# A transformer layer with 32 experts on one core: weights stored in the order of their tiles

## The chip, the core and the metric

One core of one Trainium2 chip. Its engines work beside each other and meet through semaphores: TensorE (PE, matmuls, with PEld for its weight loads), VectorE (DVE), ScalarE (ACT), GpSimd (POOL) and SyncE (SP, which here issues the transfers). Sixteen DMA engines carry data from the chip's memory (HBM) to the core's own memory. The metric is device time in microseconds.

## The reference

One layer of a diffusion transformer in float32: 256 latent tokens and 256 context tokens of width 1024. It is adaLN, two attention branches with their gates, and then a mixture of experts: the four best of 32 experts for each token.

```
def ada_params(cond, w_ada, b_ada):
    m = jax.nn.silu(cond) @ w_ada + b_ada
    return jnp.split(m, N_MOD, axis=-1)
...
def hybrid_layer(x, ctx, mod, mod_ctx, p, rope, update_ctx):
    shift1, scale1, gate1, shift2, scale2, gate2 = mod
...
    k_mla_c, v_mla_c, k_swa_c, v_swa_c = kv_side(hc, p, None)
    k_mla, v_mla, k_swa, v_swa = kv_side(h, p, rope)
    q_mla, q_swa, gate_a, gate_b = q_side(h, p, rope)
    o_a = mla_attend_latent(q_mla, k_mla, v_mla, k_mla_c, v_mla_c)
    o_b = swa_attend_latent(q_swa, k_swa, v_swa, k_swa_c, v_swa_c, p['swa_sink'])
    x_new = x + gate1[..., None, :] * merge_branches(o_a, o_b, gate_a, gate_b, p)
    x_new = x_new + gate2[..., None, :] * moe(modulate(x_new, p['norm2_g'], shift2, scale2), p)
...
def moe(h, p):
...
    def run_block(args):
        tok, e, w = args
        xb = x_pad[tok]
        act = clamped_swiglu(xb @ w_gu[e] + b_gu[e])
        return (act @ w_dn[e] + b_dn[e]) * w[:, None]
```

An expert holds a gate-and-up matrix of 1024 x 2048 and a down matrix of 1024 x 1024, 12.6 MB in float32; the 32 experts are 403 MB. The attention part reads some 55 MB more.

## The kernel before

The kernel has a **front** (adaLN, keys, values and queries, attention, merge, router) and then the 32 **experts**, each with all its weights and at most 64 tokens. Weights land in ten **frames** of 128 partitions x 4096 float32 (`frames`, in the profile `f`; a frame that gets new contents in its second life is called `g`). In the experts the load of a **slab** fills one frame: 512 rows of a matrix by 1024 columns, 2048 KB. Nine frames go round in a fixed order, `order = (2, 7, 3, 6, 8, 4, 5, 9, 1)`; an expert takes four slabs of the gate-and-up matrix and two of the down matrix. The first slabs come in two halves each (`parts=2`), and the last expert's down matrix in smaller pieces.

In memory the matrices stand row by row. A load takes rows `k0*128 ...` of some columns and puts row `k*128 + p` into partition p, so that what a partition gets is several separate runs:

```
def kslab(f, lo, w, k0, kn, c0, cn):
    return load(f, lo, w[k0 * 128:(k0 + kn) * 128, c0:c0 + cn].rearrange("(k p) n -> p k n", p=128), kn, cn)
```

A run is `cn` columns: 1024 (4 KB) in the experts' slabs, 512 (2 KB) for the output projection and for adaLN beside attention, 256 (1 KB) for the branch projections, 128 (512 B) for the gates and for the adaLN pieces of the head. In the head, adaLN comes in eight pieces `a0` to `a7` of 1 MB (two loads each), and the first columns of the input projection in pieces `v` and `q` of 256 KB. Beside attention, `ada_load` puts each of seven adaLN blocks into frame 4 (`f_67` in the order below) in two halves, DVE accumulates each with eight instructions, and `gate_load` and `br_load` put gate and branch weights into frames 2 and 3 (`f_65` and `f_66`).

The order of all instructions is found by `Program`, a list scheduler: the program is recorded in an order that is right, each instruction has a price in `price`, and the instruction with the longest path behind it goes first. It also chooses the engine of copies, scalings and subtractions that more than one engine can do (`either`). A load's price is its bytes divided by a constant. All loads are issued by SP in the order in which they were recorded, and a load that has to wait for its frame holds the loads behind it.

Of the kernel before, what the change touches and what calls it, by code (L numbers as in the profile page):

```python
# [18 lines left out]
D = 1024  # L19
# [3 lines left out]
H = 8  # L23
# [9 lines left out]
class View:  # L33
    """A tile that gets its place when the program is put in order, and the view taken of it."""
# [31 lines left out]
class Place:  # L66
    """A place on chip for new contents: its tile is made when the first instruction that touches it is issued."""
# [10 lines left out]
class Program:  # L78
    """Records the instructions of a program in an order that is right, and issues them in one that keeps every
    dependence and lets no engine wait without need: list scheduling by critical path on modelled engines."""  # L80
# [21 lines left out]
    def pool(self, slots, shared=False, ahead=8):  # L102
        """Places handed out as the order of issue is found; shared: tiles with other uses later on."""
        me = {"slots": slots, "free": [(0.0, s) for s in slots], "queue": [], "head": 0, "turn": 0, "shared": shared, "ahead": ahead}
        self.pools.append(me)
        uid = len(self.pools)

        def get():
            if self.direct:
                me["turn"] += 1  # L110
                return me["free"][me["turn"] % len(me["free"])][1]
            v = Virtual(me, f"v{uid}_{len(me['queue'])}")
            v.index = len(me["queue"])
            me["queue"].append(v)
            return View(v)

        return get
# [50 lines left out]
    def cells(self, x):  # L168
        """The tile of an access and the cells of it that it may touch."""
# [41 lines left out]
    def price(self, eng, method, args, kw):  # L211
# [3 lines left out]
        if eng == "sync":  # L215
            ap = self.concrete(out)
            b = 4
            for d in ap.shape:
                b *= d
            return b / 360.0  # L220
# [95 lines left out]
    # ---- ordering  # L316
    def order(self):
# [11 lines left out]
        def work(s, cost):  # L329
            """End of tensor engine work that starts at s: half speed in a window after one with little work."""  # L330
# [125 lines left out]
def emit(nc, tc, io, out):  # L456
# [7 lines left out]
    # ---------------------------------------------------------------- places on chip  # L464
# [34 lines left out]
    def load(f, lo, src, a, b):  # L499
        v = fv(f, lo, a * b, a)  # L500
        SY.dma_start(v, src)
        return v

    def kslab(f, lo, w, k0, kn, c0, cn):
        return load(f, lo, w[k0 * 128:(k0 + kn) * 128, c0:c0 + cn].rearrange("(k p) n -> p k n", p=128), kn, cn)
# [59 lines left out]
    # split of float32 into two float32r parts that add up to it exactly  # L565
# [29 lines left out]
    # ---------------------------------------------------------------- loads of the head  # L595
    def ada_head_load(k):
        v = fv(2 + k // 2 % 3, k % 2 * 2048, 2048)
        w = v.rearrange("p (i k n) -> p i k n", i=2, k=KT)
        for i in range(2):
            SY.dma_start(w[:, i], io["w_ada"][:, i * D + k * 128:i * D + (k + 1) * 128].rearrange("(k p) n -> p k n", p=128))  # L600
        return w
# [4 lines left out]
    def head_load(what):  # L606
# [5 lines left out]
        elif a in "vq":  # L612
            kslab({"v": 5, "q": 8}[a], i * 512, io["w_in"], i, 1, {"v": 0, "q": 928}[a], 512)
# [13 lines left out]
    # ---------------------------------------------------------------- norm of x and ctx  # L627
# [20 lines left out]
    # ---------------------------------------------------------------- adaLN shift and scale, keys and values  # L648
# [24 lines left out]
    # rope tables with the gains  # L673
# [56 lines left out]
    # ---------------------------------------------------------------- rotation  # L730
# [11 lines left out]
    # ---------------------------------------------------------------- keys, values, queries  # L742
# [27 lines left out]
    def gate_load(ci, f):  # L770
        for n in range(4):
            kslab(f, n * 1024, io["w_in"], 0, KT, 1440 + ci * 512 + n * 128, 128)

    w_lat = kslab(3, 0, io["w_in"], 0, KT, 512, 416)
    gate_load(0, 2)
    load(4, 0, io["w_kv_up"].rearrange("(k p) n -> p k n", p=128), 2, D)
    load(4, 2048, io["w_q_up"][0:256].rearrange("(k p) n -> p k n", p=128), 2, H * QK)
# [31 lines left out]
    def ada_load(ci, f=4):  # L809
        for i in range(2):  # L810
            kslab(f, i * 2048, io["w_ada"], 4 * i, 4, ci * 512, 512)
# [146 lines left out]
    # ---------------------------------------------------------------- gates and the rest of adaLN, beside attention  # L958
# [11 lines left out]
    # ---------------------------------------------------------------- attention  # L970
# [72 lines left out]
    def br_load(br, f):  # L1043
        for m in range(4):
            kslab(f, m * 1024, io[("w_branch_a", "w_branch_b")[br]], 0, 4, m * 256, 256)
# [16 lines left out]
    # position in the attention loop of gate chunks 0-3, adas 6-11, branch loads  # L1062
# [36 lines left out]
    # ---------------------------------------------------------------- branches, merge, output projection  # L1099
    for n, f in ((0, 4), (1, 5)):  # L1100
        kslab(f, 0, io["w_out"], 0, KT, n * 512, 512)
# [39 lines left out]
    # ---------------------------------------------------------------- router  # L1141
# [55 lines left out]
    # ---------------------------------------------------------------- experts  # L1197
# [11 lines left out]
    def slab(w, k0, c0, parts=1):  # L1209
        i = turn.get("slab", 0)  # L1210
        turn["slab"] = i + 1
        kn = 4 // parts
        for j in range(parts):
            kslab(order[i % len(order)], j * kn * 1024, w, k0 + j * kn, kn, c0, 1024)
# [74 lines left out]
    for e in range(E):  # L1289
# [14 lines left out]
        for pr in range(2):  # L1304
            w = [slab(io["w_gate_up"][e], 4 * i, pr * 1024, parts=1 + (e < 2)) for i in range(2)]
            gate_up(lambda k: xT[:, k, s:s + CAP], w, pr, act, lambda g, pr: bgu[:, g, e, 4 * pr:4 * pr + 4])
        if e < E - 1:
            w = [slab(io["w_down"][e], 4 * i, 0, parts=1 + (e == 0)) for i in range(2)]
# [8 lines left out]
    # the last expert: one half of the columns after the other, the last loads small  # L1317
    w = []
    for n in range(2):
        f = order[turn["slab"] % len(order)]  # L1320
        turn["slab"] += 1
        for k0, kn in ((0, 8),) if n == 0 else ((0, 4), (4, 2), (6, 2)):
            kslab(f, k0 * 512, io["w_down"][E - 1], k0, kn, n * 512, 512)
# [17 lines left out]
    # ---------------------------------------------------------------- experts chosen by more than CAP tokens  # L1341
    over = nc.values_load(cnt[0:1, 0:1], min_val=0, max_val=T)
    with tc.If(over > CAP):
# [6 lines left out]
        for lap in range(1, T // CAP):  # L1350
            with tc.For_i(0, E, 1) as e:
# [12 lines left out]
                for pr in range(2):  # L1364
                    w = [slab(io["w_gate_up"][bass.ds(e, 1)].rearrange("e d f -> (e d) f"), 4 * i, pr * 1024)
                         for i in range(2)]
                    gate_up(lambda k: xs[:, k], w, pr, act, lambda g, pr: be[:, g, 4 * pr:4 * pr + 4])
                w = [slab(io["w_down"][bass.ds(e, 1)].rearrange("e f d -> (e f) d"), 4 * i, 0) for i in range(2)]
# [14 lines left out]
def _host(i):  # L1383
# [10 lines left out]
    def tab(dim):  # L1394
# [23 lines left out]
         "x": v("x").reshape(T, D), "ctx": v("ctx").reshape(NCTX, D), "b_down": v("b_down").reshape(E, D),  # L1418
         "w_gate_up": v("w_gate_up").reshape(E, D, 2 * F), "w_down": v("w_down").reshape(E, F, D)}
    for n in ("b_ada", "w_ada", "w_in", "w_q_up", "w_kv_up", "w_branch_a", "w_branch_b", "w_out", "w_router"):  # L1420
# [20 lines left out]
```

## Time and profile before

| | |
|---|---|
| device time, median of 3 runs | 1271.77 us (1271.32 to 1273.93) |
| profiled execution, span | 1272.1 us |
| PE busy | 1152.3 us (91%) |
| DVE busy | 412.6 us (32%) |
| ACT busy | 309.1 us (24%) |
| POOL busy | 162.3 us (13%) |
| read from HBM | 457.24 MB, 360 GB/s over the span |

The span runs from the profiled execution's first instruction to its last; the page gives no other time for that execution. Busy shares are unions of the instructions' times; matmuls overlap, so a busy PE is not a PE at its peak. In the page's rows of 40 slices a digit is a busy share in tenths. The DMA share of the windows can exceed 1 a little, because packets overlap in their records.

### The profile page before, as it was taken

What the parts mean: (1) busy time and instruction counts of PE and PEld (TensorE: products, weight loads), DVE (VectorE), ACT (ScalarE), POOL (GpSimd) and SP (SyncE); (2) the same over time, 40 slices, a digit from 0 to 9 for tenths busy, and PEclk for the clock granted to TensorE, in tenths of its full rate; (3) what the DMA queues carried; (4) which work ended last, traced back from release to release, by engine and by line L of the source; (5) the groups of instructions that cost most, each with busy time, mean ns of one, the idle gap of its engine ahead of it and who ended that gap; (6) DMA issues with size and microseconds to landing.
All of it is one profiled execution on the core that took longest, in us unless ns stands there. A gap on an engine that the chain in (4) does not pass through costs nothing.

```text
span 1272.1 us, 15108 instructions
## 1 busy us (share of the span) xinstructions
PE 1152.3 (91%) x5960; PEld 548.8 (43%) x5960; DVE 412.6 (32%) x1235; ACT 309.1 (24%) x689; POOL 162.3 (13%) x131
## 2 busy tenths in 40 slices
PE   5989998998999998999999998989898989888976
PEld 3778767984433343333333333333333333333322
DVE  3599997554203122211211221111111111111122
ACT  5468775543101111111111111111111111111110
POOL 3566556570000000000000000000000000000000
PEclk9999999999999999999999999999999999999999
DMA  9964277888999999999999999999999999999994
GB/s 302 334 207 114 85 241 275 289 320 284 409 409 358 409 409 409 409 409 409 409 409 409 409 409 409 409 409 409 409 409 409 409 409 409 409 409 409 409 408 182
DMA packets 158869, 459.34 MB, mean 361 GB/s; under 512 B 6532, under 2 KB 44676, under 8 KB 158792
## 3 DMA queue, kind: packets, MB, share of 16 engines
q1 hardware_dynamic: 158792, 458.31, 93.9%
q8 instruction: 49, 0.80, 0.3%
q14 instruction: 28, 0.23, 0.0%
HBM read 457.24 MB, written 1.05 MB: 360 GB/s over the span
## 4 chain that ended last, share of the span: by engine, by line
PE 59%; DMA 25%; DVE 9%; ACT 3%; POOL 2%; issue 2%; SPq 0%; ACTq 0%; DVEq 0%; POOLq 0%
PE b L163 59%; DMA f<-in_w_gate_up_dram 10%; DMA f<-in_w_down_dram 9%; DVE w L163 5%; DVE s L163 2%; DMA g<-in_w_down_dram 2%; DMA g<-in_w_gate_up_dram 2%; ACT g L163 1%; ACT w L163 1%; DMA f<-in_w_ada_dram 1%; DVE f L163 1%; POOL s L163 1%; POOL f L163 1%; DMA f<-in_x_dram 0%; ACT f L163 0%
## 5 line engine op out<-in xcount | busy, mean ns | idle before, releaser
L163 PE MATMUL b<-f,g 128*64 128x512 f32 x2064 | 475.8, 601 | 27.4 <-DMA f<-in_w_gate_up_dram 15.6
L163 PEld LDWEIGHTS b<-f,g 128*64 128x64 f32 x2064 | 141.4, 137 | 304.6 <-issue 255.5
L163 DVE TENSOR_TENSOR w<-b,bgu 128x128 f32<-128x128 f32 x256 | 61.7, 283 | 585.3 <-PE b L163 571.3
L163 PE MATMUL b<-g,g 128*64 128x512 f32 x1008 | 229.7, 597 | 7.7 <-DMA g<-in_w_gate_up_dram 6.8
L163 PE MATMUL b<-f,f 128*128 128x256 f32 (+5 forms) x1012 | 194.6, 347 | 7.2 <-POOL f L163 2.5
L163 PE MATMUL b<-w,w 128*128 128x128 f32 (+3 forms) x904 | 153.3, 390 | 18.0 <-ACT w L163 13.3
L163 PEld LDWEIGHTS b<-f,f 128*128 128x128 f32 (+2 forms) x1012 | 150.4, 193 | 30.0 <-issue 6.5
L163 ACT ACTIVATE g<-b 128x512 f32<-128x512 f32 x68 | 40.5, 597 | 402.7 <-PE b L163 402.7
L163 PEld LDWEIGHTS b<-w,w 128*128 128x128 f32 (+3 forms) x904 | 91.9, 187 | 94.5 <-issue 53.2
L163 POOL TENSOR_TENSOR f<-f,f 128x512 fp32r<-128x512 f32 (+2 forms) x86 | 118.8, 1395 | 88.9 <-ACT f L163 65.2
L163 PEld LDWEIGHTS b<-g,g 128*64 128x64 f32 x1008 | 68.4, 136 | 140.7 <-issue 121.3
L163 ACT ACTIVATE w<-b 128x512 f32<-128x512 f32 (+3 forms) x137 | 64.2, 479 | 158.2 <-PE b L163 153.7
L163 PE MATMUL b<-consts,g 128*128 128x128 f32 x256 | 47.4, 308 | 25.8 <-ACT g L163 25.5
L163 ACT ACTIVATE g<-b,modT,G 128x128 f32<-128x128 f32 x94 | 39.4, 455 | 126.1 <-PE b L163 111.9
L163 PEld LDWEIGHTS b<-consts,g 128*128 128x128 f32 x256 | 35.5, 208 | 72.4 <-ACT g L163 53.6
L163 PE MATMUL b<-consts,w 128*128 128x128 f32 (+3 forms) x358 | 59.2, 282 | 8.2 <-DVE modT L163 2.2
L163 ACT ACTIVATE g<-w 128x256 f32<-128x256 f32 x64 | 26.4, 416 | 161.8 <-DVE w L163 161.8
L163 ACT ACTIVATE f<-f 128x512 fp32r<-128x512 f32 (+3 forms) x95 | 56.4, 605 | 38.5 <-PE b L163 17.2
L163 PEld LDWEIGHTS b<-consts,w 128*128 128x128 f32 (+1 forms) x358 | 41.4, 146 | 44.2 <-issue 24.3
L163 DVE SCALAR_TENSOR_TENSOR w<-f,sc,w 128x512 f32<-128x512 f32 x60 | 57.4, 956 | 1.9 <-DMA f<-in_w_ada_dram 1.2
L163 DVE TENSOR_SCALAR g<-b,G,modT 128x128 f32<-128x128 f32 x34 | 13.6, 409 | 112.3 <-ACT g L163 112.3
L163 DVE TENSOR_SCALAR w<-w 128x256 f32<-128x256 f32 x128 | 36.6, 288 | 2.2
(119 smaller groups left out, 499.2 us busy)
## 6 DMA issues: line engine op xcount, KB each, us to landing
f<-in_w_gate_up_dram SPq DMA_DIRECT2D x80, 2048.0 KB, 24.0
f<-in_w_down_dram SPq DMA_DIRECT2D x41, 2048.0 KB, 24.1
g<-in_w_gate_up_dram SPq DMA_DIRECT2D x40, 2048.0 KB, 24.0
g<-in_w_down_dram SPq DMA_DIRECT2D x20, 2048.0 KB, 24.0
f<-in_w_ada_dram SPq DMA_DIRECT2D x16, 1024.0 KB, 5.3
f<-in_w_gate_up_dram SPq DMA_DIRECT2D x10, 1024.0 KB, 7.5
f<-in_w_ada_dram SPq DMA_DIRECT2D x16, 512.0 KB, 7.6
f<-in_w_in_dram SPq DMA_DIRECT2D x16, 512.0 KB, 4.9
```

The costliest lines, as they stand in the source:

```text
L163: getattr(getattr(self.nc, eng), method)(*a, **k)
```

## The change

The host hands every weight over in the order of its tiles: what a partition gets in one load stands as one run. A slab of an expert becomes 128 runs of 16 KB. The adaLN pieces of the head become one load of 8 KB runs each instead of two, the two up-projections become one load, adaLN beside attention has 8 KB runs, gate and branch loads 4 KB, the output projection 16 KB. The bytes that land are the same; the last expert's down matrix is handed over a second time in its own order. The planner's price of a load changes from bytes/360 to bytes/415. Comments were taken out.

```diff
@@ class Program: price @@
-            return b / 360.0
+            return b / 415.0
@@ emit @@
-    def load(f, lo, src, a, b):
-        v = fv(f, lo, a * b, a)
-        SY.dma_start(v, src)
-        return v
-
-    def kslab(f, lo, w, k0, kn, c0, cn):
-        return load(f, lo, w[k0 * 128:(k0 + kn) * 128, c0:c0 + cn].rearrange("(k p) n -> p k n", p=128), kn, cn)
+    def flat(f, lo, src, a):
+
+        n = src.shape[-1]
+        SY.dma_start(fv(f, lo, n), src)
+        return fv(f, lo, n, a)
...
     def ada_head_load(k):
         v = fv(2 + k // 2 % 3, k % 2 * 2048, 2048)
-        w = v.rearrange("p (i k n) -> p i k n", i=2, k=KT)
-        for i in range(2):
-            SY.dma_start(w[:, i], io["w_ada"][:, i * D + k * 128:i * D + (k + 1) * 128].rearrange("(k p) n -> p k n", p=128))
-        return w
+        SY.dma_start(v, io["w_ada1"][k])
+        return v.rearrange("p (i k n) -> p i k n", i=2, k=KT)
...
-            kslab({"v": 5, "q": 8}[a], i * 512, io["w_in"], i, 1, {"v": 0, "q": 928}[a], 512)
+            flat({"v": 5, "q": 8}[a], i * 512, io["w_" + a][i], 1)
...
-            kslab(f, n * 1024, io["w_in"], 0, KT, 1440 + ci * 512 + n * 128, 128)
-
-    w_lat = kslab(3, 0, io["w_in"], 0, KT, 512, 416)
+            flat(f, n * 1024, io["w_gates"][ci, n], KT)
+
+    w_lat = flat(3, 0, io["w_lat"], KT)
     gate_load(0, 2)
-    load(4, 0, io["w_kv_up"].rearrange("(k p) n -> p k n", p=128), 2, D)
-    load(4, 2048, io["w_q_up"][0:256].rearrange("(k p) n -> p k n", p=128), 2, H * QK)
+    flat(4, 0, io["w_ups"], 1)
...
-            kslab(f, i * 2048, io["w_ada"], 4 * i, 4, ci * 512, 512)
+            flat(f, i * 2048, io["w_ada2"][ci - 4][:, i * 2048:(i + 1) * 2048], 4)
...
-            kslab(f, m * 1024, io[("w_branch_a", "w_branch_b")[br]], 0, 4, m * 256, 256)
+            flat(f, m * 1024, io["w_branch"][br, m], 4)
...
-        kslab(f, 0, io["w_out"], 0, KT, n * 512, 512)
+        flat(f, 0, io["w_out"][n], KT)
...
-    def slab(w, k0, c0, parts=1):
+    def slab(w, parts=1):
         i = turn.get("slab", 0)
         turn["slab"] = i + 1
-        kn = 4 // parts
+        n = FW // parts
         for j in range(parts):
-            kslab(order[i % len(order)], j * kn * 1024, w, k0 + j * kn, kn, c0, 1024)
+            flat(order[i % len(order)], j * n, w[:, j * n:(j + 1) * n], 1)
         return fv(order[i % len(order)], 0, FW, 4)
...
-            w = [slab(io["w_gate_up"][e], 4 * i, pr * 1024, parts=1 + (e < 2)) for i in range(2)]
+            w = [slab(io["w_gate_up"][e, 2 * pr + i], parts=1 + (e < 2)) for i in range(2)]
...
-            w = [slab(io["w_down"][e], 4 * i, 0, parts=1 + (e == 0)) for i in range(2)]
+            w = [slab(io["w_down"][e, i], parts=1 + (e == 0)) for i in range(2)]
...
-            kslab(f, k0 * 512, io["w_down"][E - 1], k0, kn, n * 512, 512)
+            flat(f, k0 * 512, io["w_down_last"][n][:, k0 * 512:(k0 + kn) * 512], kn)
@@ _host @@
+    def runs(w, rows, cols, kn):
+
+        k = rows // (128 * kn)
+        w = w.reshape(*w.shape[:-2], k, kn, 128, w.shape[-1] // cols, cols)
+        w = np.moveaxis(w, (-2, -5, -3, -4, -1), (-5, -4, -3, -2, -1))
+        return np.ascontiguousarray(w).reshape(*w.shape[:-2], kn * cols)
...
+    a["w_gate_up"] = runs(v("w_gate_up").reshape(E, D, 2 * F), D, 1024, 4).reshape(E, 4, 128, FW)
+    a["w_down"] = runs(v("w_down").reshape(E, F, D), F, 1024, 4).reshape(E, 2, 128, FW)
+    a["w_down_last"] = runs(v("w_down").reshape(E, F, D)[E - 1], F, 512, 8).reshape(2, 128, FW)
```

The new price moves instructions on every engine, which the diff does not show. On SP, beside attention, before, the loads stand as follows: gate weights (`in_w_in`) into frames 2 and 3 (`f_65`, `f_66`) and adaLN halves into frame 4 (`f_67`).

```order
L163 DMA f_65<-in_w_in_dram 128x8x128 x4
L163 DMA f_66<-in_w_in_dram 128x8x128
L163 DMA f_67<-in_w_ada_dram 128x4x512
L163 DMA f_66<-in_w_in_dram 128x8x128
L163 DMA f_67<-in_w_ada_dram 128x4x512
L163 DMA f_66<-in_w_in_dram 128x8x128
L163 DMA f_67<-in_w_ada_dram 128x4x512 x2
L163 DMA f_66<-in_w_in_dram 128x8x128
L163 DMA f_67<-in_w_ada_dram 128x4x512 x2
L163 DMA f_65<-in_w_branch_b_dram 128x4x256
```

On SP in the same place, with the change:

```order
L163 DMA f_66<-in_w_gates_dram 128x1024 x4
L163 DMA f_65<-in_w_gates_dram 128x1024 x2
L163 DMA f_67<-in_w_ada_dram 128x2048
L163 DMA f_65<-in_w_gates_dram 128x1024 x2
L163 DMA f_66<-in_w_gates_dram 128x1024 x4
L163 DMA f_65<-in_w_branch_dram 128x1024 x2
L163 DMA f_67<-in_w_ada_dram 128x2048 x3
L163 DMA f_65<-in_w_branch_dram 128x1024
L163 DMA f_67<-in_w_ada_dram 128x2048 x3
```

The second adaLN half used to stand behind one gate load; now it stands behind six gate loads and two branch loads.

On PE, late in the experts, before: `b_77` and `b_78` are the two banks of the experts' groups, `f_67` to `g_2777` slabs, `g_2726` the frame with the gathered tokens; eight matmuls of one slab stand together.

```order
L163 MATMUL b_78<-f_67,g_2726 64x512 x8
L163 MATMUL b_74<-w_91,w_88 128x512
L163 MATMUL b_76<-w_91,w_88 128x512
L163 MATMUL b_77<-f_68,g_2726 64x512 x8
L163 MATMUL b_73<-w_91,w_88 128x512
L163 MATMUL b_75<-w_91,w_88 128x512
L163 MATMUL b_77<-g_2757,g_2726 64x512 x8
L163 MATMUL b_80<-consts,g_2726 128x128 x4
L163 MATMUL b_78<-g_2777,g_2726 64x512 x8
```

On PE, late in the experts, with the change (`g_2728` and `g_2753` are slabs):

```order
L163 MATMUL b_78<-f_68,g_2723 64x512 x4
L163 MATMUL b_78<-g_2728,g_2723 64x512 x2
L163 MATMUL b_77<-g_2753,g_2723 64x512 x2
L163 MATMUL b_78<-g_2728,g_2723 64x512 x2
L163 MATMUL b_77<-g_2753,g_2723 64x512 x2
L163 MATMUL b_78<-g_2728,g_2723 64x512 x2
L163 MATMUL b_77<-g_2753,g_2723 64x512 x2
L163 MATMUL b_78<-g_2728,g_2723 64x512 x2
L163 MATMUL b_77<-g_2753,g_2723 64x512 x2
```

Two groups on two banks, of two slabs, now take turns, two matmuls at a time; in many other places of the experts too.

## Rows read from the trace of the kernel before

**Rows 1.** The page: span, two engines, slices of the span, packets, the queue.

```profile
span 1272.1 us, 15108 instructions
PE 1152.3 (91%) x5960; PEld 548.8 (43%) x5960; DVE 412.6 (32%) x1235; ACT 309.1 (24%) x689; POOL 162.3 (13%) x131
...
DMA  9964277888999999999999999999999999999994
GB/s 302 334 207 114 85 241 275 289 320 284 409 409 358 409 409 409 409 409 409 409 409 409 409 409 409 409 409 409 409 409 409 409 409 409 409 409 409 409 408 182
DMA packets 158869, 459.34 MB, mean 361 GB/s; under 512 B 6532, under 2 KB 44676, under 8 KB 158792
...
q1 hardware_dynamic: 158792, 458.31, 93.9%
```

**Rows 2.** Windows by stage: busy time (instructions), PEclk, DMA share, GB/s.

```profile
core 0: us, PE busy (x) PEld busy (x) DVE busy (x) ACT busy (x) POOL busy (x), PEclk, DMA share, GB/s
0.00:66.00 66.00, 52.00 (x317) 36.37 (x318) 30.48 (x112) 32.73 (x69) 27.52 (x27) 1.00 1.07 321
66.00:295.00 229.00, 209.21 (x1476) 175.85 (x1475) 186.66 (x433) 142.57 (x336) 134.83 (x105) 0.98 0.66 221
...
400.00:1240.00 840.00, 767.53 (x3612) 287.34 (x3612) 165.32 (x585) 116.53 (x250) 0.00 (x0) 1.00 1.03 409
1240.00:1260.00 20.00, 18.04 (x70) 6.58 (x71) 4.46 (x16) 1.43 (x3) 0.00 (x0) 1.00 0.63 239
```

**Rows 3.** Waits of PE, 295 to 1273 us: total us, times, longest us.

```profile
PE b L163 <- ACT g L163: 25.8, 40, 0.8
PE b L163 <- DMA f<-in_w_gate_up_dram: 15.6, 14, 1.5
PE b L163 <- ACT w L163: 13.6, 21, 0.8
PE b L163 <- DMA f<-in_w_down_dram: 8.0, 8, 1.9
PE b L163 <- DMA g<-in_w_gate_up_dram: 6.8, 7, 1.5
...
PE b L163 <- DMA g<-in_w_down_dram: 0.7, 2, 0.4
```

**Rows 4.** All waits of PE, 500 to 740 us.

```profile
PE b L163 <- ACT g L163: 8.0, 12, 0.8
PE b L163 <- ACT w L163: 4.7, 7, 0.8
```

**Rows 5.** Timeline of SP, from 598 us: start, duration, issues.

```profile
598.09 9.98 SPq L163 DMA_DIRECT2D f<-in_w_gate_up_dram  x2
```

**Rows 6.** Windows in which one run length fills the queue.

```profile
20.00:24.00 4.00, 3.69 (x14) 2.78 (x12) 1.34 (x6) 2.74 (x5) 2.55 (x3) 1.00 1.20 290
210.00:212.00 2.00, 1.76 (x16) 1.76 (x16) 2.00 (x7) 1.05 (x2) 0.40 (x1) 1.00 1.06 399
...
212.00:214.00 2.00, 2.00 (x20) 1.87 (x20) 1.93 (x3) 2.00 (x6) 2.00 (x2) 1.00 1.04 392
```

**Rows 7.** The page's DMA issues: KB each, median us from issue to landing.

```profile
f<-in_w_gate_up_dram SPq DMA_DIRECT2D x80, 2048.0 KB, 24.0
```

**Rows 8.** Waits of PE, 0 to 66 us, the two longest.

```profile
PE b L163 <- DMA f<-in_w_ada_dram: 7.8, 1, 7.8
PE b L163 <- ACT f L163: 4.1, 1, 4.1
```

**Rows 9.** Groups of DVE by shape, 66 to 295 us: busy, mean ns, idle before.

```profile
L163 DVE SCALAR_TENSOR_TENSOR w<-f,sc,w 128x512 f32<-128x512 f32 x60 | 57.4, 956 | 1.9 <-DMA f<-in_w_ada_dram 1.2
...
L163 DVE TENSOR_TENSOR f<-f,f 128x512 fp32r<-128x512 f32 x10 | 7.5, 753 | 3.8 <-ACT f L163 3.7
```

More of the change, by code (lines that the diff above doesn't have):

```diff
@@ L1364, in emit @@
                 for pr in range(2):
-                    w = [slab(io["w_gate_up"][bass.ds(e, 1)].rearrange("e d f -> (e d) f"), 4 * i, pr * 1024)
+                    w = [slab(io["w_gate_up"][bass.ds(e, 1), 2 * pr + i].rearrange("e p f -> (e p) f"))
                          for i in range(2)]
                     gate_up(lambda k: xs[:, k], w, pr, act, lambda g, pr: be[:, g, 4 * pr:4 * pr + 4])
-                w = [slab(io["w_down"][bass.ds(e, 1)].rearrange("e f d -> (e f) d"), 4 * i, 0) for i in range(2)]
+                w = [slab(io["w_down"][bass.ds(e, 1), i].rearrange("e p d -> (e p) d")) for i in range(2)]
                 dn = down(act, w)
@@ L1417, in _host @@
          "bgu": np.ascontiguousarray(v("b_gate_up").reshape(E, 8, 128, 2).transpose(2, 3, 0, 1)),
-         "x": v("x").reshape(T, D), "ctx": v("ctx").reshape(NCTX, D), "b_down": v("b_down").reshape(E, D),
-         "w_gate_up": v("w_gate_up").reshape(E, D, 2 * F), "w_down": v("w_down").reshape(E, F, D)}
-    for n in ("b_ada", "w_ada", "w_in", "w_q_up", "w_kv_up", "w_branch_a", "w_branch_b", "w_out", "w_router"):
+         "x": v("x").reshape(T, D), "ctx": v("ctx").reshape(NCTX, D), "b_down": v("b_down").reshape(E, D)}
+    def runs(w, rows, cols, kn):
[3 more added lines that the diff above has]
+        return np.ascontiguousarray(w).reshape(*w.shape[:-2], kn * cols)
+    m = lambda n: v(n).reshape(v(n).shape[-2:])
+    w_in = m("w_in")
+    a["w_gate_up"] = runs(v("w_gate_up").reshape(E, D, 2 * F), D, 1024, 4).reshape(E, 4, 128, FW)
+    a["w_down"] = runs(v("w_down").reshape(E, F, D), F, 1024, 4).reshape(E, 2, 128, FW)
+    a["w_down_last"] = runs(v("w_down").reshape(E, F, D)[E - 1], F, 512, 8).reshape(2, 128, FW)
+    ada = runs(m("w_ada"), D, 128, 8).reshape(48, 128, 1024)
+    a["w_ada1"] = np.ascontiguousarray(ada[:16].reshape(2, 8, 128, 1024).transpose(1, 2, 0, 3)).reshape(8, 128, 2048)
+    a["w_ada2"] = runs(m("w_ada")[:, 2 * D:], D, 512, 8).reshape(8, 128, FW)
+    a["w_v"] = runs(w_in[:, :512], D, 512, 1).reshape(8, 128, 512)
+    a["w_q"] = runs(w_in[:, 928:1440], D, 512, 1).reshape(8, 128, 512)
+    a["w_lat"] = runs(w_in[:, 512:928], D, 416, 8).reshape(128, 8 * 416)
+    a["w_gates"] = runs(w_in[:, 1440:], D, 128, 8).reshape(4, 4, 128, 1024)
+    a["w_ups"] = np.concatenate([runs(m("w_kv_up"), 256, 1024, 2).reshape(128, 2048),
+                                 runs(m("w_q_up")[:256], 256, 768, 2).reshape(128, 1536)], 1)
+    a["w_branch"] = np.stack([runs(m(n), 512, 256, 4).reshape(4, 128, 1024) for n in ("w_branch_a", "w_branch_b")])
+    a["w_out"] = runs(m("w_out"), D, 512, 8).reshape(2, 128, FW)
+    for n in ("b_ada", "w_q_up", "w_router"):
         w = v(n)
```

## The prediction

> **What bounds the kernel now.** I read the page first for the span, the busy shares and the DMA line [rows 1]. PE is busy for 91% of the span and the DMA row shows 9 in nearly every slice from the middle on, so the page alone does not tell which of the two sets the end. The windows by stage separate them [rows 2]. From 0 to 66 us the DMA share is 1.07 at only 321 GB/s. From 66 to 295 us the share is 0.66 and DVE is busy 186.7 of 229 us: that stretch is not limited by transfers. From 400 to 1240 us the DMA engines move 409 GB/s without a gap, and from 1240 to 1260 us they move the rest (239 GB/s x 20 us = 4.78 MB, 11.7 us at 409). The experts' weights are thus one stream of 840 + 11.7 = 851.7 us that never stands still.
>
> The waits of PE say when that stream is what ends last. Between 500 and 740 us PE waits for ACT alone and for no transfer [rows 4]: it still has slabs that landed earlier. Over the whole expert stretch its waits for the four groups of weight loads add up to 15.6 + 8.0 + 6.8 + 0.7 = 31.1 us [rows 3], so all of them lie outside 500 to 740, and the DMA stream sets the pace of the last 500 us. SP confirms it: from 598 us an issue takes about 5 us, one after the other [rows 5], which is the time of one 2048 KB slab (2.097 MB / 409 GB/s = 5.13 us); SP has free frames and waits for the queue. A slab lands 24.0 us after its issue [rows 7], 4.7 slabs deep. Not the frames, not PE, but the rate of the DMA engines bounds this stretch.
>
> **What the change does to that rate.** It changes no byte of what the experts load, only the length of the runs: a slab is now 512 runs of 4 KB, and becomes 128 runs of 16 KB. The trace holds the rate at three run lengths [rows 6 and 2]: 512 B (adaLN pieces, 20 to 24 us) 290 GB/s; 2 KB (output projection and adaLN, 210 to 214 us) 399 and 392 GB/s; 4 KB 409 GB/s. As time of one run on one of 16 engines (16 x bytes / rate) that is 28.2 ns, 82.1 to 83.6 ns, and 160.2 ns. A run costs a start plus its bytes, and each pair of points gives the start and, extended, the time of a 16 KB run:
> - 512 B and 4 KB: slope 132.0 / 3584 = 0.03683 ns per byte, start 9.3 ns, 16 KB in 612.8 ns: 428 GB/s.
> - 2 KB at 392 and 4 KB: slope 0.0374, start 7.0 ns, 619.8 ns: 423 GB/s.
> - 2 KB at 399 and 4 KB: slope 0.0381, start 4.0 ns, 628.7 ns: 417 GB/s.
>
> No row has a run over 4 KB from this queue (it moved 158,792 packets, and 158,792 are under 8 KB [rows 1]), so this is an extension by a factor of four. I take 423, the middle of the three. The stream then takes 851.7 x 409 / 423 = 823.5 us: **28.2 us less**. The ends are 417 (835.3 us, 16.4 less) and 428 (813.9 us, 37.8 less).
>
> A rule speaks against any gain. The Trainium skill ("DMA: Bandwidth & Descriptors", section "Where 436 GB/s comes from") has the memory's share per core, about 358 GB/s, bind a transfer from HBM; by it run length would not matter and the time would stay near 1272 us. The trace disagrees: 409 GB/s for 840 us.
>
> **Does PE let the gain through?** With before's order of matmuls it could give back at most its 31.1 us of waits for loads, so 28.2 would just fit and 37.8 would not. But the new order differs. The price of a load in the planner falls by 13%, and PE's rows in the experts now alternate two groups on two banks where before ran eight matmuls of one group at a time. Before, PE waits 25.8 + 13.6 = 39.4 us for ACT to empty a finished group [rows 3]; an alternating order has other work there, so PE's own need falls as well. I count nothing for that, since PE is not the bound, but I take it that PE doesn't cap the gain. The alternation has a price: a group waits in PE's queue behind one whose slab lands later, up to one slab, 5 us, and once only, at the end; I leave it at 0 to 3 us inside the range.
>
> **The front.** Up to 66 us PE's waits are 7.8 us for the first adaLN load and 4.1 us for the normalised x behind ACT [rows 8]; after those it runs. That first load is 1 MB of 512 B runs, 3.6 us at 290 GB/s; in 8 KB runs (9.3 + 301.7 = 311 ns, 421 GB/s) 2.5 us: 1.1 us less. The x rows are 4 KB already. All other loads of the head land under PE's work. From 66 to 295 us nothing waits for loads to speak of: DVE's largest group, 60 adaLN accumulations, is 57.4 us with 1.9 us of idle time ahead of it [rows 9]. But the cheaper price moves instructions everywhere there: five more 128x512 subtractions stand on DVE (753 ns each [rows 9], 3.8 us) and five fewer on POOL. DVE has 42 us idle in that stretch, so I count 0, with 8 us either way. **Front: 1 us less.** The number of issues on SP falls by nine and costs nothing, since SP waits for the queue.
>
> **Sum.** The profiled execution's span is 1272.1 us, 0.3 above the median of the runs. 1272.1 - 28.2 - 1 = 1242.9, less 0.3: **1242 us**.
>
> **Rivals.**
> 1. The rate rises less. The 2 KB windows scatter by 7 GB/s and their upper one gives a start of only 4.0 ns. With a start of 2 to 4 ns, four runs of 160.2 ns save three starts, 6 to 12 ns of 640.8: 413 to 417 GB/s, 8 to 16 us less. About 1258 us. The Trainium skill (same page, "Why small descriptors are slow") gives a fixed cost of about 3 cycles per packet, 3.5 ns at the page's 850 MHz: its estimate would be 416 GB/s, some 14 us less and 1256 us. The 290 GB/s of 512 B runs speak against so small a start: 512 B at 4 KB's pace plus 4 ns would be 24 ns, and they take 28.2.
> 2. Nothing happens: a 16 KB run is cut to pieces of 4 KB or less on its way. For it: no longer packet is in this queue's record. The stream keeps 409 GB/s, and the front's 1 us is left: 1271 us, give or take the 8 of the front.
> 3. Slower: adaLN loads come late. On SP the second load into the adaLN frame f_67 now stands behind six gate loads and two branch loads instead of one gate load, and SP issues in order; whoever waits for a frame holds all behind. DVE's 57.4 us of accumulations hang on these loads. If they slide to the end of attention, the experts start later by what DVE can't overlap. It decides from 31 us when the rate rises to 423, from 3.5 us when it doesn't; the ceiling is 57 us. Against it: DVE's order places the accumulations among the softmax steps as before. With a delay of 40 us: 1282 us.
>
> **How the numbers follow.** Forecast (417 to 428 GB/s, front within 8 us): chance 0.68, its own range 1230 to 1256. Rival 1: 0.10. Rival 2: 0.11. Rival 3: 0.06. A front earlier by more than 8 us, with the rate risen: 0.05, about 1225. A range of 1229 to 1264 holds the forecast and rival 1, and leaves out rivals 2 and 3 and half of the last, 0.2 in all. A measurement of this kernel tells 0.2% (2.5 us) from no change. Faster: 0.68 + 0.10 + 0.05, and 0.02 of rival 2: 0.85. Same: 0.04. Slower: 0.05 of rival 2 and rival 3: 0.11.
>
> **What would show it.** Right: a flat stretch after 400 us at 417 to 428 GB/s; slabs landing in about 23 us instead of 24.0; issues on SP 4.95 us apart; packets of 16 KB in the queue's line, about a quarter as many in all; PE's waits for ACT falling below 39.4 us. Wrong: a flat rate of 409, which means rival 2; a rate that rose with holes in the DMA row, which means that PE or the frames became the bound; a first expert matmul well off 299 us, which means that the reordering of the front weighed more than I gave it.

## The result, and the profile after

The changed kernel takes 1251.24 us (median of 4 runs, 1250.38 to 1252.2) where the kernel before took 1272.42 beside it: a ratio of 0.983, interval 0.9816 to 0.9844, 21 us faster. The prediction was 1242, its range 1229 to 1264. The sum missed by 9 us, and it did so with two errors of opposite sign, which the profile separates at one point: the first matmul of an expert. About 2 us of the 9 are neither: the sum took 0.3 us off the span to get to a median, but the device time of an execution stands some 2 us above its span (1251.48 for the span of 1249.7 below).

The timeline of PE shows that matmul in the kernel before (columns: start, duration, what):

```profile
299.48 2.02 PE L163 MATMUL b<-f,g 128*64 128x512 f32 x8 [0.33 <-ACT g L163]
```

and in the changed kernel:

```profile
314.44 2.02 PE L163 MATMUL b<-f,g 128*64 128x512 f32 x8 [0.33 <-ACT g L163]
```

The spans are 1272.1 and 1249.7 us. So the experts took 972.6 us and take 935.3, **37.3 less**, where the prediction had 28.2; and the front takes 299.5 us and then 314.4, **14.9 more**, where it had 1 less. 37.3 - 14.9 = 22.4, the difference of the two spans.

The page after, its rates and packets, to be read against [rows 1]:

```profile
span 1249.7 us, 15145 instructions
...
GB/s 360 386 110 93 78 167 218 323 257 365 290 422 429 426 428 407 428 427 393 428 427 427 427 428 402 428 428 428 427 428 427 428 429 427 427 428 427 427 428 167
DMA packets 43524, 459.33 MB, mean 368 GB/s; under 512 B 6388, under 2 KB 6644, under 8 KB 14008
...
q1 hardware_dynamic: 43448, 458.31, 88.7%
```

The flat 409 has become 426 to 429 GB/s with dips to 407, 393 and 402, and the same megabytes go in 43,524 packets instead of 158,869. The windows after, of the stages of [rows 2] (columns as there):

```profile
0.00:66.00 66.00, 52.99 (x315) 36.09 (x316) 32.78 (x111) 31.64 (x69) 25.49 (x25) 1.00 0.94 365
66.00:295.00 229.00, 203.84 (x1414) 170.53 (x1412) 180.56 (x407) 137.88 (x324) 122.63 (x97) 0.96 0.52 188
...
400.00:1240.00 840.00, 796.71 (x3755) 307.37 (x3752) 168.37 (x599) 121.03 (x271) 0.00 (x0) 0.97 0.99 419
```

From 66 to 295 us PE, DVE and ACT have each done less work than before in the same time (DVE 180.56 for 186.66): the front is late on all three. POOL's fall is no sign of that, since work has moved away from it. PE's granted clock has fallen in the front (0.98 to 0.96) and in the experts (1.00 to 0.97).

The waits of PE in the experts after, against [rows 3]:

```profile
PE b L163 <- ACT g L163: 25.7, 12, 2.6
PE b L163 <- DVE g L163: 6.2, 3, 3.2
PE b L163 <- DMA f<-in_w_gate_up_dram: 6.0, 3, 3.3
...
PE b L163 <- ACT w L163: 4.7, 17, 0.5
...
PE b L163 <- DMA g<-in_w_gate_up_dram: 1.3, 1, 1.3
```

Of 31.1 us of waits for loads 7.3 are left. The waits for ACT are 30.4 us instead of 39.4, but g makes fewer and longer ones: 12 of up to 2.6 us, not 40 of up to 0.8. (These rows begin at 295 us, inside the late front; from 314 us on the waits for ACT are 27.9 us.)

SP's timeline after, around 750 us (start, duration, issues), shows what the stream waits for at a dip:

```profile
735.98 0.33 SPq L163 DMA_DIRECT2D f<-in_w_gate_up_dram  x1
758.81 4.62 SPq L163 DMA_DIRECT2D g<-in_w_gate_up_dram  x2
763.48 0.43 SPq L163 DMA_DIRECT2D f<-in_w_gate_up_dram  x1
763.96 0.95 SPq L163 DMA_DIRECT2D f<-in_w_down_dram  x2
```

```profile
755.00:770.00 15.00, 14.74 (x78) 6.80 (x76) 6.40 (x25) 2.69 (x6) 0.00 (x0) 1.00 0.96 376
```

Before, one issue took some 5 us because the queue held it [rows 5]. Now an issue often takes a fraction of a microsecond; here SP then stands for 22 us until PE has read a frame, and five issues follow at once. The rate falls to 376 GB/s around the end of that gap. So in such places the frames, and behind them PE, hold the loads. It is not so everywhere: an equal gap of SP from 910 to 932 us leaves 428 GB/s between 905 and 940, where the loads issued ahead cover it, and from 800 to 1220 us no dip is left.

### The profile page after: what moved, and what is told of

Read it like the earlier page. It is cut to its first block, busy times and chain, and to the rows that moved or that the text cites. A ratio compares the mean times of both kernels' runs of the same rounds, so it can differ in the third digit from the quotient of the medians.

```text
span 1249.7 us, 15145 instructions
## 1 busy us (share of the span) xinstructions
PE 1153.1 (92%) x5960; PEld 558.9 (45%) x5960; DVE 410.6 (33%) x1227; ACT 309.8 (25%) x703; POOL 151.1 (12%) x125
## 2 busy tenths in 40 slices
DMA packets 43524, 459.33 MB, mean 368 GB/s; under 512 B 6388, under 2 KB 6644, under 8 KB 14008
## 4 chain that ended last, share of the span: by engine, by line
PE 74%; DMA 11%; DVE 10%; ACT 2%; issue 2%; POOL 1%; SPq 0%; DVEq 0%; ACTq 0%; POOLq 0%
PE b L163 74%; DMA f<-in_w_gate_up_dram 8%; DVE w L163 6%; DVE f L163 2%; DVE s L163 1%; ACT w L163 1%; DMA f<-in_w_ada_dram 1%; DMA w<-in_cos_s_dram 1%; DMA f<-in_ctx_dram 1%; ACT g L163 1%; POOL f L163 1%; SPq L163 0%; POOL rq_s L163 0%; ACT f L163 0%; POOL s L163 0%
## 5 line engine op out<-in xcount | busy, mean ns | idle before, releaser
L163 PEld LDWEIGHTS b<-f,g 128*64 128x64 f32 x2064 | 146.1, 140 | 317.3 <-issue 265.9
L163 PE MATMUL b<-g,g 128*64 128x512 f32 x1008 | 235.3, 609 | 12.2 <-ACT g L163 7.8
L163 PE MATMUL b<-f,f 128*128 128x256 f32 (+5 forms) x1012 | 197.6, 351 | 15.9 <-POOL f L163 5.5
L163 PEld LDWEIGHTS b<-g,g 128*64 128x64 f32 x1008 | 71.0, 139 | 152.4 <-issue 129.6
L163 POOL TENSOR_TENSOR f<-f,f 128x512 fp32r<-128x512 f32 (+2 forms) x81 | 111.2, 1386 | 109.3 <-ACT f L163 86.6
L163 ACT ACTIVATE w<-b 128x512 f32<-128x512 f32 (+4 forms) x137 | 62.6, 480 | 165.7 <-PE b L163 164.9
L163 DVE TENSOR_SCALAR w<-consts,posm,s 128x64 f32<-128x64 f32 x64 | 16.6, 309 | 144.8 <-PE b L163 144.8
L163 ACT ACTIVATE g<-b,modT,G 128x128 f32<-128x128 f32 x107 | 42.5, 453 | 65.2 <-PE b L163 57.1
L163 DVE TENSOR_SCALAR w<-consts,posm,wts 128x128 f32<-128x128 f32 x64 | 18.0, 341 | 120.1 <-PE b L163 120.1
L163 DVE TENSOR_SCALAR g<-b,G,modT 128x128 f32<-128x128 f32 x21 | 8.4, 409 | 145.1 <-ACT g L163 145.1
## 6 DMA issues: line engine op xcount, KB each, us to landing
f<-in_w_gate_up_dram SPq DMA_DIRECT2D x80, 2048.0 KB, 20.4
```

What stands on the lines that cost most here:

```text
L163: getattr(getattr(self.nc, eng), method)(*a, **k)
```

## The experiments

Two halves were to be told apart: the rate of the stream and what PE lets through, and the late front. All times are against the kernel before on the same chip (1272 to 1274 us).

### The experts' layout alone

The kernel before, with only the experts' weights in tile order; the loads of the front and the price stay, and so every engine's order stays that of before. Of its edit the line of the gate-and-up matrix:

```diff
-            w = [slab(io["w_gate_up"][e], 4 * i, pr * 1024, parts=1 + (e < 2)) for i in range(2)]
+            w = [slab(io["w_gate_up"][e, 2 * pr + i], parts=1 + (e < 2)) for i in range(2)]
```

> Only the experts' weights are handed over in tile order; front loads and the price of 360 stay as before, and so does every instruction's place. Theory P (long runs raise the rate of the stream from 409 to 428 GB/s, and the price of 415 delays the front by some 15 us): first expert matmul at 299 to 301 us, a flat 428 GB/s, PE's waits for loads down from 31.1 us to under 6, about 1241 us (31 us less; the order of before cannot give back more). Rival Q (the front of the changed kernel is late because of the new layout of its loads): the same here, about 1241. Rival R (the gain of the experts came from the alternating order, not from the rate): 1262 us or more, with the rate up and holes in the stream.

1236.09 us, ratio 0.9711 (0.9695 to 0.9727). Its window in the steady part, and its waits of PE from 280 us on:

```profile
400.00:1200.00 800.00, 757.86 (x3596) 284.89 (x3592) 161.18 (x578) 115.85 (x249) 0.00 (x0) 1.00 1.01 428
```

```profile
PE b L163 <- ACT g L163: 26.1, 41, 0.8
PE b L163 <- ACT w L163: 14.4, 23, 0.8
...
PE b L163 <- DMA f<-in_w_gate_up_dram: 0.2, 1, 0.2
```

The first expert matmul stands at 299.0 us, as before. The span falls by 37.9 us with PE's order untouched (the medians by 36.6), and PE's waits for loads fall from 31.1 to 0.2 us while those for ACT stay. That is 5 us more than the 31 that theory P allowed, so its limit on the order of before has fallen; rival R falls too, since the order did not change. The layout of the experts alone is worth more than the whole change.

The windows from the first expert matmul to the end, before and then here, show where the 37.4 us of the experts come from:

```profile
299.48:1272.10 972.62, 887.19 (x4152) 333.23 (x4152) 191.80 (x673) 133.32 (x285) 0.00 (x0) 0.99 1.00 397
```

```profile
299.01:1234.20 935.19, 881.67 (x4152) 332.08 (x4152) 192.13 (x673) 133.25 (x285) 0.00 (x0) 0.99 0.98 412
```

PE's idle time falls by 31.9 us, nearly all of it the waits for loads; the other 5.5 us are busy time of the same 4152 matmuls at the same mean clock. PE's timeline shows one such place, 32 matmuls of one group before and here:

```profile
1235.42 3.65 PE L163 MATMUL b<-g,g 128*64 128x512 f32 x16
1240.15 3.65 PE L163 MATMUL b<-g,g 128*64 128x512 f32 x16 [1.08 <-DMA g<-in_w_gate_up_dram]
```

```profile
1200.29 7.09 PE L163 MATMUL b<-g,g 128*64 128x512 f32 x32
```

Broken by a wait they take 2 x 3.65 = 7.30 us besides the wait, unbroken 7.09: this break costs 0.21 us more. Of 31 waits for loads one is left, so an estimate for all is 30 x 0.21 = 6.3 us, near the 5.5.

### The changed kernel at the old price, and the new price alone

The changed kernel with the price set back:

```diff
-            return b / 415.0
+            return b / 360.0
```

> The changed kernel with the price of a load at bytes/360. Theory P: first expert matmul back at 296 to 302 us instead of 314, experts in the order of before, 1236 to 1243 us. Rival Q: first expert matmul stays near 314 us, 1253 to 1257 us.

1244.65 us, ratio 0.9782 (0.9766 to 0.9798). First expert matmul at 306.8 us: half of the delay has gone, and neither theory's window (296 to 302, or near 314) holds it. What is left of it at the price of before comes with the front's loads, which are cut differently (16 halves of adaLN pieces are 8 loads, two up-projections one), and with the order that follows from that.

The reverse, the kernel before with the price 415 and nothing else:

```diff
-            return b / 360.0
+            return b / 415.0
```

> The kernel before with the price of a load at bytes/415 and nothing else. Theory P: first expert matmul at 310 to 318 us, stream flat at 409 GB/s, 1283 to 1290 us, slower than before. Rival Q: first expert matmul near 300 us, 1270 to 1274 us. Rival R: the alternating order alone makes it faster, 1255 us or less.

1294.19 us, ratio 1.0171 (1.0154 to 1.0188): slower than before by 22 us. Both the time and the first expert matmul lie above theory P's numbers and rule out Q and R:

```profile
321.52 2.02 PE L163 MATMUL b<-f,g 128*64 128x512 f32 x8 [0.33 <-ACT g L163]
```

The price alone costs that, and the experts gain little from the new order (968.6 us from there to the end, for 972.6), as PE's waits show:

```profile
PE b L163 <- DMA f<-in_w_gate_up_dram: 30.2, 16, 5.3
PE b L163 <- DMA g<-in_w_gate_up_dram: 20.9, 9, 5.3
PE b L163 <- ACT g L163: 10.1, 6, 2.6
...
PE b L163 <- ACT w L163: 4.7, 17, 0.5
```

The alternating order took the waits for ACT down from 39.4 to 14.8 us, and those for loads rose to 51.1: at 409 GB/s the stream sets the end, and the waits only change their name.

### The whole layout with the order kept

The changed kernel at price 360, its adaLN pieces and up-projections issued in as many loads as before, so that the scheduler finds the order of before (the line of the price is left out here):

```diff
-        SY.dma_start(v, io["w_ada1"][k])
+        for i in range(2):
+            SY.dma_start(v[:, i * 1024:(i + 1) * 1024], io["w_ada1"][k][:, i * 1024:(i + 1) * 1024])
...
-    flat(4, 0, io["w_ups"], 1)
+    flat(4, 0, io["w_ups"][:, :2048], 1)
+    flat(4, 2048, io["w_ups"][:, 2048:], 1)
```

> The whole new layout, but with the price of 360 and with the adaLN pieces and the up-projections loaded in as many loads as before, so that every instruction stands where it stood in the kernel before. If the front's delay comes from the order alone (P), the new layout of the front's loads can only help: first expert matmul at 294 to 299 us, flat 428 GB/s, 1230 to 1236 us. If the new layout itself delays the front (Q): first expert matmul at 303 to 314 us, 1240 us or more.

1235.04 us, ratio 0.9707 (0.9694 to 0.972), and the first expert matmul 1.6 us earlier than before:

```profile
297.84 2.02 PE L163 MATMUL b<-f,g 128*64 128x512 f32 x8 [0.27 <-ACT g L163]
```

The instructions of PE, DVE, ACT and POOL stand in the trace in the order of before, one by one. So the long runs of the front are worth 1 to 2 us, as the prediction had it, and all the rest of what happened to the front is order.

### Other prices

The experts' layout alone, at price 340 and at 440:

```diff
-            return b / 360.0
+            return b / 340.0
```

> The experts' layout alone (as in the first experiment) with the price at bytes/340. If the front's order simply suffers under a cheaper price of loads, a dearer one leaves the first expert matmul at 299 us or earlier, 1236 us or less. If the planner's offsets fit the price of 360 alone, any other price delays it: 303 to 320 us, 1240 to 1256 us.

1238.02 us, one run, first expert matmul at 299.4. That the order fits 360 alone has fallen: a dearer load does the front no harm. The time is 2 us over the 1236 that was named; from the first expert matmul to the end it takes 936.8 us, for 935.2.

```diff
-            return b / 360.0
+            return b / 440.0
```

> The experts' layout alone with the price at bytes/440. If a cheaper price delays the front steadily: first expert matmul at 321 us (as with 415 and the old layout) or later, 1256 us or more. If the delay is a matter of chance for each price: anywhere between 299 and 325 us.

1262.26 us, one run, first expert matmul at 316.3. A cheaper load costs, but not in proportion: 415 alone gave 321.5. That fits the second expectation, a matter of chance for each price, and not a steady delay.

### Whose price it is

The experts' layout alone, with 415 for the experts' loads and 360 for those of the front:

```diff
+            name = str(getattr(self.concrete(args[1]).tensor, "name", ""))
-            return b / 360.0
+            return b / (415.0 if "w_gate_up" in name or "w_down" in name else 360.0)
```

> The kernel before with the experts' weights alone in tile order; the price is 415 for the experts' loads only and 360 for all loads of the front. Theory S (the late front comes from the price of the front's own loads): first expert matmul at 298 to 301 us as before, experts in the alternating order of the changed kernel, so about 935 us from there to the end, median 1234 to 1238. Theory T (a dearer or cheaper price of the experts' loads moves the front too): first expert matmul at 312 or later, about 1250. Theory U (the alternating order alone makes PE's need smaller): the expert stretch under 930 us; against it (half-clock stretches give the saved waits back): 933 to 938 us and a mean granted clock of 0.97 to 0.98 in the steady stretch, where the kernel with price 360 has 1.00.

1233.71 us, ratio 0.9696 (0.968 to 0.9712); first expert matmul at 298.3, 932.6 us from there to the end. Theory S is right for the front. On the experts neither U nor its counterpart is met by its numbers: 932.6 us lies just below 933 to 938 and above 930. The order of before takes 935.2 and 934.8 us there (layout alone, order kept) and the changed kernel, which alternates too, 935.3; so the alternating order brings between 0 and 2.6 us, and the clock of 0.98 that was named with the counterpart is there.

With the two prices exchanged:

```diff
+            return b / (360.0 if "w_gate_up" in name or "w_down" in name else 415.0)
```

> The mirror image: 415 for the loads of the front, 360 for those of the experts. Theory S: first expert matmul at 314 to 322 us, experts in the sequential order with a granted clock of 1.00, about 935 us to the end, time 1250 to 1258. Theory T: first expert matmul at 298 to 303, time 1235 to 1239.

1262.13 us, one run:

```profile
324.80 2.02 PE L163 MATMUL b<-f,g 128*64 128x512 f32 x8 [0.33 <-ACT g L163]
```

That lies a little above the 314 to 322 us of theory S, as the time does above its 1250 to 1258, and far from T's 298 to 303. The price of the front's own loads makes the front late.

### adaLN ahead

The changed kernel, with the adaLN jobs beside attention given a longer path by hand.

```diff
-        prog.lean = Q["lean"].get(key, 0.0)
+        prog.lean = Q["lean"].get(key, 0.0) + (60000.0 if key in ('ada4', 'ada5', 'ada6', 'ada7', 'ada8', 'ada9', 'ada10', 'ada11') else 0.0)
```

> The changed kernel, price 415, with the adaLN jobs beside attention given a longer path by hand, so that the second adaLN load into its frame stands behind four gate loads and ahead of the branch loads. If the late adaLN loads are what delays the front, DVE's last adaLN accumulation comes by 242 us instead of 251.7, the first expert matmul by 307 and the time is 1244 or less. If the delay is spread over the whole order of the front, the first expert matmul stays at 312 or later and the time at 1248 or more, even where the accumulations end sooner.

1245.11 us, one run, and the first expert matmul at 308.0, each about 1 us above the first expectation's numbers; the last adaLN accumulation of DVE ends at 227.1 us instead of 251.7 (235.7 before). SP's timeline of the changed kernel from 109 us shows what was late:

```profile
109.33 0.33 SPq L163 DMA_DIRECT2D f<-in_w_ada_dram  x1
111.89 33.84 SPq L163 DMA_DIRECT2D f<-in_w_gates_dram  x6
149.55 7.00 SPq L163 DMA_DIRECT2D f<-in_w_branch_dram  x2
163.03 15.54 SPq L163 DMA_DIRECT2D f<-in_w_ada_dram  x3
```

and with adaLN ahead:

```profile
101.28 0.33 SPq L163 DMA_DIRECT2D f<-in_w_ada_dram  x1
107.84 29.19 SPq L163 DMA_DIRECT2D f<-in_w_gates_dram  x4
139.93 8.08 SPq L163 DMA_DIRECT2D f<-in_w_ada_dram  x2
```

The second adaLN load stands at 163 us behind six gate and two branch loads in the one, at 140 us in the other (141.7 before). DVE's work between 110 and 150 us follows it; the windows of before, of the changed kernel and of this one, in that order:

```profile
110.00:150.00 40.00, 37.49 (x270) 32.18 (x269) 38.46 (x117) 30.96 (x79) 20.09 (x19) 1.00 0.40 116
```

```profile
110.00:150.00 40.00, 35.69 (x269) 30.99 (x268) 26.29 (x74) 25.98 (x62) 19.80 (x17) 1.00 0.31 106
```

```profile
110.00:150.00 40.00, 36.45 (x271) 30.73 (x270) 35.34 (x100) 29.71 (x74) 18.61 (x16) 1.00 0.25 82
```

DVE is busy 38.46 us, then 26.29, then 35.34. So the late adaLN loads are rival 3 of the prediction, real but smaller. Bringing them ahead gave back 6.4 of the 14.9 us, with whatever else moved in the order; 8.5 are left, though here adaLN ends earlier than before.

The two figures need not be two parts of a sum. The chain of work that ended last in the changed kernel runs through an adaLN load late in the front (start, duration):

```profile
219.71 6.68 DMA f<-in_w_ada_dram
```

And in ten of the fourteen kernels, before and the changed one among them, the first expert matmul comes 62.8 to 64.0 us after DVE's last adaLN accumulation, whether that ends at 233.1 or at 261.2 us. In the changed kernel adaLN ends 16.0 us later than before and the experts start 14.9 later. In the other four (price 360 with the new cut, prices 340 and 440, adaLN ahead) the distance is 70 to 81 us, so something else ends last there. That speaks for late adaLN as the limit of the changed kernel and for a second limit, 8.5 us later than before, just beneath it; that adaLN sets the start in each of the ten is not shown. How PE's time up to the first expert divides is read from one window in each, of before, of the changed kernel and of this one:

```profile
0.00:299.50 299.50, 265.10 (x1810) 215.58 (x1810) 220.82 (x563) 175.76 (x404) 162.35 (x131) 0.98 0.76 246
```

```profile
0.00:314.40 314.40, 271.48 (x1808) 218.25 (x1808) 223.97 (x567) 175.56 (x405) 151.15 (x125) 0.96 0.63 235
```

```profile
0.00:308.00 308.00, 270.02 (x1809) 215.74 (x1809) 222.57 (x558) 175.04 (x411) 151.30 (x126) 0.97 0.65 240
```

PE does the same 1808 to 1810 matmuls in all three and is busy 265.1, 271.5 and 270.0 us, idle 34.4, 42.9 and 38.0. With adaLN ahead 3.6 us more idle time and 4.9 us more busy time than before are left. A lower granted clock (0.97 and 0.96 for 0.98) goes with the longer busy time; that it is the whole of it was not tested.

### The run length by itself

The changed kernel with each slab stored in two blocks, so that a run is 8 KB, and in eight blocks, 2 KB; the order of all instructions is the same. Of each edit only the line that stores the gate-and-up matrix is shown; the down matrix and the loads follow it.

```diff
+    a["w_gate_up"] = runs(v("w_gate_up").reshape(E, D, 2 * F), D, 1024, 4).reshape(E, 4, 128, 2, FW // 2).transpose(0, 1, 3, 2, 4)
```

> The changed kernel with the experts' slabs stored in two blocks, so that a slab is 256 runs of 8 KB instead of 128 of 16 KB; every instruction keeps its place. A start of 9.3 ns for each run and 0.03683 ns per byte (512 B and 4 KB of the kernel before) give 311 ns, 421 GB/s flat, and a stream some 13 us longer: 1252 to 1263 us. If the rate depends on something other than a start per run (such as where runs lie in memory), 8 KB runs in blocks of 1 MB stay at 428 GB/s or fall to 409.

```diff
+    a["w_gate_up"] = runs(v("w_gate_up").reshape(E, D, 2 * F), D, 1024, 4).reshape(E, 4, 128, 8, FW // 8).transpose(0, 1, 3, 2, 4)
```

> The changed kernel with the experts' slabs stored in eight blocks: 1024 runs of 2 KB for each slab, every instruction in its place. A start of 9.3 ns and 0.03683 ns per byte give 84.7 ns, 387 GB/s flat; the stream of some 350 MB then takes some 85 us more than at 428: 1325 to 1340 us.

1260.78 and 1341.71 us, one run each; the second is 1.7 us above what was expected. The windows of the steady part, 8 KB and then 2 KB:

```profile
400.00:1200.00 800.00, 753.76 (x3562) 292.82 (x3560) 154.25 (x559) 115.73 (x260) 0.00 (x0) 0.97 1.01 421
```

```profile
400.00:1200.00 800.00, 697.63 (x3240) 268.52 (x3238) 145.32 (x527) 105.07 (x237) 0.00 (x0) 0.95 1.05 386
```

With 409 at 4 KB [rows 2] and 428 at 16 KB (the first experiment) the rate is 386, 409, 421 and 428 GB/s. A start of 9.3 ns and 0.03683 ns per byte, the prediction's first pair of points, gives 387, 409, 421 and 428.

### The version that the runs point to

The whole layout with the order kept (above), and the price of the experts' loads alone set to 415:

```diff
+            return b / (415.0 if "w_gate_up" in name or "w_down" in name else 360.0)
```

> The version the runs point to: every weight in tile order, the loads of the front cut and priced (360) as before, so that the front's order is that of before, and 415 for the experts' loads alone. If the parts add up: first expert matmul at 297.8 us as with the order kept, 932.6 us from there to the end as with the split price, span 1230.4, median 1231 to 1234. If the alternating order of the experts is worth nothing by itself: 1234 to 1236, as with the order kept at price 360.

1232.57 us, ratio 0.9679 (0.9663 to 0.9695), span 1230.3 us. The first expert matmul stands at 297.1 us. The parts add up, and its median is the lowest of all: 41 us below the kernel before (1273.62 beside it). Against the same layout at 360 throughout the gain is 2.5 us, and the two intervals just touch; from the experts' layout with the same two prices (1233.71) it can't be told apart.

## Why the prediction was right, and where it was not

**The bound of before: right.** The stream of the experts' weights was what ended last. With the experts' runs at 16 KB and nothing else changed, the waits for loads went from 31.1 to 0.2 us and the span fell by 37.9.

**The rate: the mechanism right, the size too small.** The prediction took 423 GB/s, the middle of three pairs; it is 428, the upper one, from the longest and the shortest run of the kernel before. The two lower pairs rested on windows of 2 us in the front with 392 and 399 GB/s, but 2 KB runs in a steady stream move 386: the short windows read high, and the start came out too small. The term was 28.2 us and measured 37.3. Rival 1 fell with it: the start per run is 9.3 ns here. Rival 2 fell on the rate and on the packets, a quarter as many. The estimate after the Trainium skill ("DMA: Bandwidth & Descriptors", section "Why small descriptors are slow") fell too: it gave 416 GB/s with a start of 3.5 ns. As a limit on this one core, the Trainium skill's memory share of 358 GB/s (the same title, section "Where 436 GB/s comes from") is contradicted further, by 428 GB/s over 800 us.

**PE as a cap: the limit read too low, the reason given half wrong.** The prediction said that with before's order PE could give back at most 31.1 us, so that 37.8 would not fit. The first experiment gave 37.9 with that order. So the sum of PE's waits for loads is no upper limit to what faster loads save: a wait also breaks PE's run of matmuls, 0.21 us at the place shown, and 5.5 of the 37.4 us in the experts were busy time. It also said that PE's own need falls, since the alternating order has other work during ACT's. It falls by little. Eight experts in the changed kernel, and eight in the kernel with the order of before and the same layout (the first experiment):

```profile
545.50:776.90 231.40, 220.00 (x1042) 84.93 (x1040) 45.37 (x164) 33.84 (x76) 0.00 (x0) 0.97 1.00 420
```

```profile
533.70:766.00 232.30, 218.76 (x1044) 81.79 (x1042) 46.66 (x168) 33.73 (x72) 0.00 (x0) 1.00 1.01 427
```

The idle time falls from 13.5 to 11.4 us and the busy time rises from 218.8 to 220.0: 0.9 us less for eight experts, 3.6 if all 32 were like these. The largest group of PE in these two stretches (count, busy us, mean ns, idle time ahead) shows where the rise is, the changed kernel first:

```profile
L163 PE MATMUL b<-f,g 128*64 128x512 f32 x514 | 120.2, 617 | 7.8 <-ACT g L163 7.8
```

```profile
L163 PE MATMUL b<-f,g 128*64 128x512 f32 x514 | 116.9, 598 | 0.0
```

The same 514 matmuls take 3.3 us longer, at a granted clock of 0.97 for 1.00 (what PE did before it fell is in the last section). So part of the saved waiting goes with the lower clock. PE and the loads now need nearly the same time: eight experts' weights are 100.7 MB, 235 us at 428 GB/s, against PE's 231.4, and the slabs that had landed ahead make up the rest.

**The front: the step that failed.** It was "I count 0, with 8 us either way" for the moved instructions, on the ground that DVE has 42 us idle. It measured 14.9 us later. The price alone makes the front 22 us later (321.5), the front's new loads at the old price 7 (306.8), and both together 14.9: they do not add, and each change of an input gives another order. In the six kernels whose front loads are cut as before and priced at 360 or less the first expert matmul stands at 297.1 to 299.5 us, in the eight others at 306.8 to 324.8. DVE's own work up to the first expert grew by only 3.2 us (224.0 for 220.8), which the 3.8 us of moved subtractions cover. The idle share of DVE was no cover: 40 of its 42 us before are waits for PE, ACT, POOL and one load, so DVE was idle where its next input had not arrived. The late adaLN loads, which the prediction had as rival 3 with a threshold of 31 us and 0.06, came in below that threshold and together with the gain; with them brought ahead the front is 6.4 us earlier. What holds the other 8.5 us then, more idle time of PE and a lower clock spread over the front, was not traced to a single wait, and that stays open.

**Luck.** Either error alone would have kept the time inside the range: with the rate as predicted and the front as measured the sum is 1258.5, with the rate as measured and the front as predicted 1233.5. That 1242 came within 9 us is luck: they cancel in part.

**The checks that it named.** Flat at 417 to 428: yes, with dips. Landing in about 23 us: the profile's page says 20.4 to 22.0, as the queue is kept less full (24.9 in the first experiment, at the same rate). Issues 4.95 us apart: no, they come in bunches after waits for a frame. A quarter of the packets, and fewer waits for ACT: yes. "A first expert matmul well off 299 us" was named as the sign of this very error, and it is what happened. One sentence ahead of the prediction is not right: the loads stand on SP not simply as recorded, but in the order in which the scheduler's clock makes them ready, which is why a price moves them.

## What to carry to other kernels

A transfer that a queue's start per run slows down can be priced from two run lengths that lie far apart and fill the queue for long; a window of 2 us is no such row. Where a list scheduler sets the order, a constant in its prices is a change of its own: apply it alone (here +22 us) and the layout alone (here -37 us), and look at the first instruction of each stage, not at the sum. A better estimate of a price (415 is nearer to the measured rate than 360) need not give a better order.

## What the runs showed of the hardware

The rate of one queue by its run length, 386, 409, 421 and 428 GB/s at 2, 4, 8 and 16 KB, follows one straight line in time per run: 9.3 ns and 0.03683 ns per byte.

A wait of PE can cost more than its own length. In the first experiment a wait of 1.08 us cost 0.21 us on top. A longer one here cost clock: in the timeline of PE after, from 500 to 1010 us, the alternating order waits once in two experts for ACT, and what follows runs slowly:

```profile
566.04 8.78 PE L163 MATMUL b<-f,g 128*64 128x512 f32 x32 [2.60 <-ACT g L163]
...
596.47 8.80 PE L163 MATMUL b<-f,g 128*64 128x512 f32 x40
```

After 2.60 us of waiting 32 matmuls take 8.78 us, where 40 of the same kind take 8.80 elsewhere. Two windows of equal length just behind the wait show why:

```profile
566.20:569.60 3.40, 3.40 (x10) 0.97 (x10) 0.60 (x2) 0.00 (x0) 0.00 (x0) 0.50 1.04 443
569.60:573.00 3.40, 3.40 (x20) 1.11 (x18) 0.00 (x0) 0.00 (x0) 0.00 (x0) 1.00 0.97 414
```

The granted clock is 0.50 in the first (1.2 instead of 2.4 GHz) and 10 matmuls go through, 20 in the second at 1.00. The ten that are missing are 1.7 us: a wait of 2.6 us cost 4.3. The order of before, whose waits for ACT are at most 0.8 us, has a mean clock of 1.00 from 400 to 1200 us (first experiment), though these waits add up to more (39.4 us from the first expert matmul on, against 27.9).
